# A decoder layer on one core: output projection of two blocks per weight group, residual in DRAM by pair, FFN operands and S5's second half at other planned times

## The chip, the cores and the metric

The kernel runs on one core of a Trainium2 chip. Five engines work side by side, each through its own instructions in a fixed order: TensorE (PE, with its weight loads PEld), VectorE (DVE), ScalarE (ACT), GpSimd (POOL) and SyncE (SP), which here issues nearly all DMA transfers. They meet through semaphores. The metric is the device time of one execution in microseconds.

## The reference

One layer over 2048 positions with 1024 channels. The input is normalised and projected. 512 columns go through S5 (32 groups, each a complex diagonal state, then GELU and a sigmoid GLU), the rest through an RG-LRU with a gate. Both outputs are normalised and projected together, the residual is added, and a SwiGLU FFN follows. The part that the change touches, shortened:

```python
z = jax.nn.gelu(y)                                  # y: S5's output
z = z * jax.nn.sigmoid(z @ w_glu + b_glu)           # the GLU
...
mix = jnp.concatenate([rms_norm(s5_out, s5_out_g), rms_norm(lru_out, lru_out_g)], axis=-1)
x = x + mix @ w_out
h2 = rms_norm(x, norm2_g)
x = x + (jax.nn.silu(h2 @ w_gate) * (h2 @ w_up)) @ w_down
return rms_norm(x, final_g)
```

All is in fp32. A product of fp32 operands is made of three matmuls: each operand is split in a high part and a remainder, and high by high, high by remainder and remainder by high are summed in PSUM.

## The kernel before, in words

**Tiling and stages.** Channels lie on the partitions. Positions go in four blocks of 512 (b = 0 to 3). For each block `in_tb` makes the input projection, the RG-LRU and S5's input. S5 runs twice, g = 0 for blocks 0 and 1, g = 1 for blocks 2 and 3, eight steps each: `s5_in`, `s5_scan`, `s5_out`; `s5_u` loads its input, `s5_z` stores its output to the DRAM tensor `zb`. Then `glu_tb(b)` makes the GLU of a block and its normalised mix, and `out_tb(b)` the output projection. The FFN works on pairs of blocks with a Winograd form of seven products (j = 1 to 7) on sums and differences of operand quarters.

**What sets the order.** Python code writes events with planned times (`at(t, fn)`) in units in which a product of three matmuls is PT = 0.65. The events are sorted by this time; a scheduler in the building layer then places each engine's instructions by its own model of when they are ready. So a planned time is a wish, and the order that comes out is fixed before the program runs.

**Around the change.** `Unit` (L152 to L205) loads a weight tile in parts of four chunks (`wraw`), splits each part on ACT (`whi`, L188) and on DVE or POOL (`wlo`, L189). `out_tb(b, t0)` makes eight units for the eight output chunks m, with 24 matmuls each (L214), out of the operands that `pair(b)` names: `areaH`/`areaL` (tiles `aH`, `aL`, in pool Q) for even blocks, `actH`/`actL` (pool A) for odd ones. Each product ends in one of two PSUM banks `acc`. L968 adds the residual `xc`, `SumSq` squares and sums it, and the result goes to the DRAM tensor `x1d`; at the end the row scale goes to `r2d`. The blocks follow one another: GLU 0 and 1, projection 0 and 1, GLU 2 and 3, projection 2 and 3. In `glu_tb`, `zsplit` splits GELU's output into `pair(b)`, and `mix(k)` writes the normalised operand k (0 to 3 from S5, 4 to 7 from the RG-LRU) to the same tiles: a DVE instruction (`nf`, L299), an ACT cast (L300) and a subtraction on DVE or POOL (L301).

The FFN's first operands come from `x_first(0, t)`: for k = 0 to 3, `combos` loads two chunks of `x1d` for both blocks of the pair and the row scales (three tiles `hx`, L1053 and L1055), normalises them (L1059), builds the Winograd sums `ht`, and `split_x2` splits them into `xh`, `xl`. `x_ahead(1)` does the same for the second pair later and stores the results to `xcd`. All these tiles belong to pool D1, which `open_d1` opens after it has closed pools L, Q and S; D1 takes over their space, and each tile waits until what lay there has been read.

Of the kernel before, what the change touches and what calls it, by code (L numbers as in the profile page):

```python
# [79 lines left out]
def build(tc, nc, I, O, ctx):  # L80
# [44 lines left out]
    x1d = dram("x1d", (DM, SEQ))  # L125
    r2d = dram("r2d", (SEQ,))
# [111 lines left out]
    class SumSq:  # L238
# [24 lines left out]
        @staticmethod  # L263
        def spread(y, dst=None):
            ps = aux("nm")
            if dst is not None:
# [4 lines left out]
                return
            for i in range(4):
                PE.matmul(ps[:, 128 * i:128 * i + 128], lhsT=y[:, i:i + 1].to_broadcast([128, 128]), rhs=eye,
                          start=True, stop=True)
# [593 lines left out]
    for g, (ts, dt) in enumerate(((ts0, 10), (tP1 - 10.0, 7))):  # L868
# [18 lines left out]
    def glu_tb(b, t0):  # L887
# [52 lines left out]
        t = t0 + 16 * PT  # L940

# [4 lines left out]
        for i, k in enumerate((4, 5, 6, 7)):  # L946
            at(max(t0 + 6.0, t2s) + 0.5 * i, lambda k=k: mix(k))
        at(t + 6.0, lambda: cur.__setitem__("rs", cur["ss"].finish()))
        for k in range(4):
            at(t + 7.0 + 0.5 * k, lambda k=k: mix(k))  # L950

    def out_tb(b, t0):
        cur = C[b]
        ss = SumSq(8, dv=b == NB - 1)
        for m in range(8):
            t = t0 + m * 8 * PT
            u = Unit(t, I["w_out"][m], 8, GP if m % 3 == 1 else DV)

            def prod(m=m, u=u):
                cur["o", m] = acc()  # L960
                mm3(cur["o", m], u, [(k, k) for k in range(8)], *pair(b), True, True)

            at(t - 5, lambda m=m: cur.__setitem__(("x", m), load_chunk(xT, b, m)))
            at(t, prod)

            def post(m=m):
                xc = cur.pop(("x", m))
                DV.tensor_tensor(out=xc, in0=cur.pop(("o", m)), in1=xc, op=ALU.add)  # L968
                ss.add(xc)
                SP.dma_start(x1d[128 * m:128 * m + 128, b * TB:(b + 1) * TB], xc)  # L970
# [10 lines left out]
    for kind, b in (("g", 1), ("o", 0), ("o", 1), ("g", 2), ("g", 3), ("o", 2), ("o", 3)):  # L981
        if kind == "g":
            glu_tb(b, T)
            T += 16 * PT
        else:
            out_tb(b, T)
            T += 64 * PT
# [57 lines left out]
    def combos(p, k, t):  # L1045

        o = 2 * TB * p
        cur = {}

        def load():  # L1050
            for i in range(2):
                cur[i] = d1("hx", 3, w=2 * TB)
                SP.dma_start(cur[i], x1d[128 * (k + 4 * i):128 * (k + 4 * i) + 128, o:o + 2 * TB])  # L1053
            rs = cur["rs"] = d1("hx", 3, w=2 * TB)
            SP.dma_start(rs, r2d[o:o + 2 * TB].unsqueeze(0).to_broadcast([128, 2 * TB]))  # L1055
# [184 lines left out]
    def down(t0):  # L1240
# [287 lines left out]
```

## Time and profile before

| | |
|---|---|
| median of 3 runs | 2169.43 us (2167.53 to 2169.79) |
| the profiled execution | 2175.18 us, span 2173.4 us |
| mean granted TensorE clock in it | 0.955 |
| input projections, RG-LRU, S5's first half and the start of its second | to about 440 us |
| S5's second half, GLU 1, first products of the projection | 440 to 600 |
| projection 0 and 1, GLU 2 and 3, projection 2 and 3 | 500 to 778 |
| FFN, gate and up, then down | from 778 |

The profile gives busy time per engine in a stretch, the granted TensorE clock (1.00 is full speed), and for each instruction the idle time before it and what ended it, in brackets. A wait on an engine other than TensorE matters only where TensorE runs out of work because of it.

### The profile page before, as it was taken

Reading aid. Unit: us, or ns where it says so; the run is one execution under the profiler, and the core shown is the slowest. Engines: PE = TensorE matmul, PEld = TensorE weight load, DVE = VectorE, ACT = ScalarE, POOL = GpSimd, SP = SyncE. Lnnn points to the kernel's source line nnn. Section 1 sums busy time; section 2 is a strip of 40 time slices with the busy share of each in tenths; the row PEclk is TensorE's granted clock in tenths of the full one; section 3 lists DMA queues with packets and bytes.
Section 4 is the critical chain, followed back from the end, with each engine's and each line's share of the span. In section 5 each row is a group of like instructions: output and inputs, shape, how many; then the busy total and the mean of one; then the engine's idle time right before and its main releaser. Section 6 shows DMA issues by size and latency. Waiting matters only on the chain.

```text
span 2173.4 us, 26158 instructions
## 1 busy us (share of the span) xinstructions
PE 1956.8 (90%) x8600; PEld 1564.3 (72%) x8600; DVE 1244.8 (57%) x1920; ACT 815.4 (38%) x1340; POOL 1042.6 (48%) x855
## 2 busy tenths in 40 slices
PE   6758989877898968899999989999999999999996
PEld 4536767666776756677777777777777788888785
DVE  5997658488856586444444464444444536554644
ACT  4534653563354342232332342232332344333331
POOL 1576236468834468545545552312313336544442
PEclk8968999988998989999999999999999999999998
DMA  7746998874772888644444574444443569854633
GB/s 293 218 153 190 297 248 273 226 179 142 226 209 94 257 264 279 200 146 146 160 146 143 172 235 134 149 131 136 145 131 126 189 224 317 279 184 135 232 102 102
DMA packets 264423, 413.61 MB, mean 190 GB/s; under 512 B 60736, under 2 KB 82528, under 8 KB 264288
## 3 DMA queue, kind: packets, MB, share of 16 engines
q1 hardware_dynamic: 264288, 411.95, 59.7%
q8 instruction: 67, 1.10, 0.2%
q14 instruction: 68, 0.56, 0.1%
HBM read 288.89 MB, written 122.96 MB: 189 GB/s over the span
## 4 chain that ended last, share of the span: by engine, by line
PE 55%; DVE 4%; DMA 4%; POOL 3%; issue 2%; ACT 1%; SPq 0%; POOLq 0%; DVEq 0%; ACTq 0%
PE gt L1184 9%; PE acc L1184 9%; PE y L1184 9%; PE v L1184 5%; PE nm L1184 5%; PE y L1324 4%; PE acc L1324 4%; PE gt L1324 4%; PE v L1324 2%; PE nm L1324 2%; PE acc L214 2%; DVE wlo L1024 1%; DMA ht<-xcd 1%; DVE hx L1059 1%; DMA wraw<-w_down 1%
## 5 line engine op out<-in xcount | busy, mean ns | idle before, releaser
L1197 POOL TENSOR_TENSOR t<-t 128x512 f32<-128x512 f32 x66 | 100.8, 1527 | 348.9 <-DVE t L1223 219.4
L214 PE MATMUL acc<-actH,whi 128*128 128x512 f32 x528 | 220.0, 418 | 43.5 <-DVE gy L710 12.1
L1023 ACT CAST whi<-ws 128x512 fp32r<-128x512 f32 x176 | 109.2, 621 | 346.9 <-PE y L1184 90.4
L214 PE MATMUL acc<-actL,whi 128*128 128x512 f32 x528 | 217.5, 413 | 18.8 <-DVE actL L294 17.8
L214 PE MATMUL acc<-actH,wlo 128*128 128x512 f32 x528 | 216.9, 412 | 6.9 <-DMA wlo<-wlc 6.9
L1024 DVE TENSOR_TENSOR wlo<-ht,whi 128x512 fp32r<-128x512 f32 x112 | 107.1, 957 | 126.3 <-ACT whi L1023 122.1
L214 PEld LDWEIGHTS acc<-actH,whi 128*128 128x128 f32 x528 | 105.9, 201 | 73.8 <-issue 24.8
L1023 ACT CAST whi<-ht 128x512 fp32r<-128x512 f32 x154 | 95.1, 619 | 169.9 <-PE nm L1324 69.5
L1024 DVE TENSOR_TENSOR wlo<-ws,whi 128x512 fp32r<-128x512 f32 x176 | 134.1, 762 | 33.7 <-ACT whi L1023 33.6
L1024 DVE TENSOR_TENSOR wlo<-wraw,whi 128x512 fp32r<-128x512 f32 x88 | 72.0, 818 | 142.2 <-ACT whi L1023 142.2
L1184 PE MATMUL y<-xh,whi 128*128 128x512 f32 x308 | 124.7, 405 | 16.2 <-ACT t L1216 12.0
L214 PEld LDWEIGHTS acc<-actL,whi 128*128 128x128 f32 x528 | 105.1, 199 | 46.7 <-DVE actL L294 24.7
L1024 POOL TENSOR_TENSOR wlo<-ht,whi 128x512 fp32r<-128x512 f32 x42 | 57.9, 1379 | 158.9 <-ACT whi L1023 158.9
L1184 PE MATMUL acc<-xh,wlo 128*128 128x512 f32 x308 | 122.3, 397 | 9.6 <-DVE wlo L1024 9.6
L214 PEld LDWEIGHTS acc<-actH,wlo 128*128 128x128 f32 x528 | 105.2, 199 | 30.6 <-DMA wlo<-wlc 7.4
L1184 PE MATMUL acc<-xh,whi 128*128 128x512 f32 x308 | 122.4, 397 | 4.6 <-ACT xh L1023 3.3
L1184 PE MATMUL y<-xl,whi 128*128 128x512 f32 x308 | 123.3, 400 | 3.5 <-DVE xl L1024 3.5
L1184 PE MATMUL y<-xh,wlo 128*128 128x512 f32 x308 | 123.3, 400 | 2.9 <-DVE wlo L1024 2.9
L1184 PE MATMUL acc<-xl,whi 128*128 128x512 f32 x308 | 122.2, 397 | 1.7 <-DVE xl L1024 1.7
L1184 PE MATMUL gt<-xh,whi 128*128 128x512 f32 x308 | 121.4, 394 | 0.0
L1184 PE MATMUL gt<-xh,wlo 128*128 128x512 f32 x308 | 121.3, 394 | 0.0
L1184 PE MATMUL gt<-xl,whi 128*128 128x512 f32 x308 | 121.2, 394 | 0.0
(416 smaller groups left out, 5308.0 us busy)
## 6 DMA issues: line engine op xcount, KB each, us to landing
td<-t SPq DMA_DIRECT2D x154, 256.0 KB, 2.2
ht<-td SPq DMA_DIRECT2D x154, 256.0 KB, 3.0
wraw<-w_down SPq DMA_DIRECT2D x99, 256.0 KB, 4.5
wraw<-w_in SPq DMA_DIRECT2D x96, 256.0 KB, 5.2
scd<-ws SPq DMA_DIRECT2D x88, 256.0 KB, 2.1
ws<-scd SPq DMA_DIRECT2D x88, 256.0 KB, 2.6
wlo<-wlc SPq DMA_DIRECT2D x72, 256.0 KB, 4.4
wraw<-w_out SPq DMA_DIRECT2D x64, 256.0 KB, 4.5
```

What stands on the lines that cost most here:

```text
L214: PE.matmul(ps, lhsT=part[w][:, kw % 4, :], rhs=r_(x(kx)), start=first and i == 0 and j == 0, stop=last and i == n - 1 and j == 2)
L1023: AC.copy(hi, raw)
L1024: eng.tensor_tensor(out=lo, in0=raw, in1=hi.bitcast(F32), op=ALU.subtract)
L1059: DV.scalar_tensor_tensor(out=cur[i], in0=cur[i], scalar=pc("g2", k + 4 * i), in1=cur["rs"], op0=ALU.mult, op1=ALU.mult)
L1184: PE.matmul(ps, lhsT=a[:, k, :], rhs=x, start=j in FIRST and k == 0 and i == 0, stop=k == 3 and i == 2, skip_group_check=True)
L1197: (DV if q == 0 else GP).tensor_tensor(out=g, in0=c, in1=g, op=ALU.mult)
L1324: PE.matmul(BK[p][i], lhsT=a[:, i, :], rhs=x, start=j in FIRST and s == 0 and v == 0, stop=s == NSL - 1 and v == 2, skip_group_check=True)
```

## The change

`out_tb` becomes `out_pair(b0, t0)`. It makes the eight units of `w_out` once for two blocks. For blocks 0 and 1 the products go: chunks 0 and 1 of block 0, chunks 0 and 1 of block 1, then chunks 2 to 5 with the blocks alternating; after a planned gap of 32 PT, in which `glu_tb(2)` and `glu_tb(3)` stand, chunks 6 and 7 of block 0, then of block 1. For blocks 2 and 3 chunks 0 and 1 go the same way and chunks 2 to 7 alternate. Products end in four banks, two `acc` and two `gt`, in pairs. Each block has its own sum tile (`sum`, `sumh`); `rs` has two buffers instead of three.

`x1d` and `r2d` become two DRAM tensors each, one for a pair. GLU 2 and 3 split GELU's output into a tile `zhl` of its own (tag `u8`, one buffer, S5's input tile before), since `pair(b)` is still being read; their mix has a planned time `tm` after products 6 and 7. The RG-LRU operands of odd blocks take the tags `T` and `ig`. S5's second half is planned 16 later (tP1 + 6 instead of tP1 - 10), `open_d1` and `x_first(0)` 128 PT ahead of the FFN instead of 64.

```diff
-    for g, (ts, dt) in enumerate(((ts0, 10), (tP1 - 10.0, 7))):
+    for g, (ts, dt) in enumerate(((ts0, 10), (tP1 + 6.0, 7))):
...
+        def zpair():
+            if b < 2:
+                return pair(b)
+            if "zhl" not in cur:
+                zz = bt("u8", (128, 2, 4, TB))
+                cur["zhl"] = tuple((lambda k, i=i: zz[:, i, k, :]) for i in range(2))
+            return cur["zhl"]
...
-            at(max(t0 + 6.0, t2s) + 0.5 * i, lambda k=k: mix(k))
+            at((max(t0 + 6.0, t2s) if b < 2 else tm - 2.0) + 0.5 * i, lambda k=k: mix(k))
...
+    def out_bank():
+        n = last["bank"] = last.get("bank", -1) + 1
+        return acc() if n % 4 < 2 else aux("gt", 2)
+
+    def out_pair(b0, t0):
+        sums = {b: SumSq(8, ("sum", "sumh")[b % 2], dv=b >= NB - 2) for b in (b0, b0 + 1)}
+        blocks = (b0, b0 + 1)
+        order = [(m, b) for b in blocks for m in (0, 1)]
+        order += [(m, b) for m in range(2, 6 if b0 == 0 else 8) for b in blocks]
+        if b0 == 0:
+            order += [(m, b) for b in blocks for m in (6, 7)]
+        units = {}
+        for n, (m, b) in enumerate(order):
+            cur = C[b]
+            t = t0 + n * 8 * PT + (32 * PT if b0 == 0 and n >= 12 else 0)
+            if m not in units:
+                units[m] = Unit(t, I["w_out"][m], 8, GP if m % 3 == 1 else DV)
...
+    glu_tb(1, T)
+    T += 16 * PT
+    out_pair(0, T)
+    tg = T + 96 * PT
+    glu_tb(2, tg, T + (128 + 16 + 1) * PT)
+    glu_tb(3, tg + 16 * PT, T + (128 + 32 + 1) * PT)
+    T += 128 * PT + 32 * PT
+    out_pair(2, T)
+    T += 128 * PT
...
-    at(tC - 64 * PT + 4.0, open_d1)
+    at(tC - 128 * PT + 4.0, open_d1)
     at(tC + 1.0, open_d2)
-    x_first(0, tC - 64 * PT + 12.0)
+    x_first(0, tC - 128 * PT + 12.0)
```

Three places in the order that comes out. First TensorE where the first two products end, before (`acc_4508` is chunk 1 of block 0, `acc_4634` its chunk 2; `y` and `v` are steps of S5):

```order
L863 MATMUL y_4389<-u8_3797,mo_4196 128x128
L259 MATMUL nm_4541<-ones_62,sumg_4335 128x1 x4
L214 MATMUL acc_4400<-aL3_4104,whi_4355 128x512
L214 MATMUL acc_4400<-aH3_4102,wlo_4356 128x512
L214 MATMUL acc_4508<-aL3_4104,whi_4475 128x512
L214 MATMUL acc_4508<-aH3_4102,wlo_4476 128x512
L801 MATMUL v_4485<-u8_3797,mi_4479 64x128 x8
L214 MATMUL acc_4634<-aH0_3624,whi_4504 128x512
L214 MATMUL acc_4634<-aL0_3626,whi_4504 128x512
```

and now, where `gt_4480` and `gt_4553` are chunks 0 and 1 of block 1:

```order
L863 MATMUL y_4542<-u8_3983,mo_4346 128x128
L801 MATMUL v_4628<-u8_3983,mi_4624 64x128 x8
L214 MATMUL gt_4480<-actH_70,whi_4126 128x512
L214 MATMUL gt_4553<-actH_70,whi_4239 128x512
L214 MATMUL gt_4480<-actL_71,whi_4126 128x512
L214 MATMUL gt_4480<-actH_70,wlo_4127 128x512
```

The third product was block 0's and is now block 1's, in other banks, and its first matmuls alternate with the fourth's. Second DVE, before, at block 3's first product (`xc_6116` takes it out of its bank, `xc_6160` is the second's; `hx`, `xl10`, `ht` belong to `x_first`, k = 0):

```order
L968 TENSOR_TENSOR xc_6116<-acc_6135,xc_6116 128x512
L189 TENSOR_TENSOR wlo_6242<-wraw_6118,whi_6241 128x512
L1059 SCALAR_TENSOR_TENSOR hx_6245<-hx_6245,par_61,hx_6249 128x1024
L1059 SCALAR_TENSOR_TENSOR hx_6247<-hx_6247,par_61,hx_6249 128x1024
L226 TENSOR_SCALAR nv_6180<-nm_6175 128x4
L1024 TENSOR_TENSOR xl10_6314<-hx_6245,xh10_6313 128x512
L1068 TENSOR_TENSOR ht_6298<-hx_6247,hx_6245 128x512
L228 TENSOR_SCALAR nv_6180<-nv_6180 128x4
L189 TENSOR_TENSOR wlo_6254<-wraw_6129,whi_6253 128x512
L1069 TENSOR_TENSOR ht_6299<-ht_6298,hx_6245 128x512
L229 TENSOR_SCALAR nv_6180<-nv_6180 128x4
L1024 TENSOR_TENSOR xl70_6326<-ht_6298,xh70_6325 128x512
```

and now, where `acc_6332` is chunk 6 of block 3, `gt_6374` and `gt_6416` are chunk 7 of blocks 2 and 3, the last product:

```order
L990 TENSOR_TENSOR xc_6319<-acc_6332,xc_6319 128x512
L253 TENSOR_TENSOR sumh_5875<-sumh_5875,sq_6402 128x512
L990 TENSOR_TENSOR xc_6359<-gt_6374,xc_6359 128x512
L253 TENSOR_TENSOR sum_5760<-sum_5760,sq_6442 128x512
L990 TENSOR_TENSOR xc_6399<-gt_6416,xc_6399 128x512
L1082 SCALAR_TENSOR_TENSOR hx_5763<-hx_5763,par_61,hx_5767 128x1024
L1082 SCALAR_TENSOR_TENSOR hx_5765<-hx_5765,par_61,hx_5767 128x1024
L226 TENSOR_SCALAR nv_6458<-nm_6453 128x4
L253 TENSOR_TENSOR sumh_5875<-sumh_5875,sq_6494 128x512
L1048 TENSOR_TENSOR xl10_5820<-hx_5763,xh10_5819 128x512
```

`x_first` stood between block 3's products and now stands behind all of them. Third SP at the same place, before:

```order
L182 DMA wraw_6173<-w_out 128x512
L1053 DMA hx_6245<-x1d_84 128x1024
L1053 DMA hx_6247<-x1d_84 128x1024
L970 DMA x1d_84<-xc_6072 128x512
L1055 DMA hx_6249<-r2d_85 128x1024
L182 DMA wraw_6235<-w_out 128x512
```

and now:

```order
L992 DMA x1d1_85<-xc_6319 128x512
L1076 DMA hx_5763<-x1d0_84 128x1024
L1076 DMA hx_5765<-x1d0_84 128x1024
L1078 DMA hx_5767<-r2d0_86 128x1024
L1155 DMA rd_6361<-w_gate 128x512
L992 DMA x1d1_85<-xc_6359 128x512
```

`xc_6072` is block 2's eighth product, `xc_6319` block 3's seventh: the loads stood ahead of the store of block 2's last product, with block 3's eight still to come, and now stand behind the store of the third product from the end.

More of the change, by code (lines that the diff above doesn't have):

```diff
@@ L124, in build @@
     lrud = dram("lrud", (512, SEQ))
-    x1d = dram("x1d", (DM, SEQ))
-    r2d = dram("r2d", (SEQ,))
+    x1d = [dram(f"x1d{i}", (DM, 2 * TB)) for i in range(2)]
+    r2d = [dram(f"r2d{i}", (2 * TB,)) for i in range(2)]
     xcd = dram("xcd", (2, 4, 128, 7, TB))
@@ L926, in prod @@
                     mm3(cur["ps", 2 * uu + i], u, [(4 * i + k, k) for k in range(4)],
-                        *pair(b), True, True)
+                        *zpair(), True, True)
             at(t, prod)
@@ L940, in glu_tb @@
         t = t0 + 16 * PT
+        tm = t + 7.0 if tm is None else tm
         def mix(k):
@@ L946, in glu_tb @@
         for i, k in enumerate((4, 5, 6, 7)):
-            at(max(t0 + 6.0, t2s) + 0.5 * i, lambda k=k: mix(k))
+            at((max(t0 + 6.0, t2s) if b < 2 else tm - 2.0) + 0.5 * i, lambda k=k: mix(k))
         at(t + 6.0, lambda: cur.__setitem__("rs", cur["ss"].finish()))
         for k in range(4):
[L950 to L960, printed above, removed]
+            at(tm + 0.5 * k, lambda k=k: mix(k))
@@ L961, in prod, with post @@
                 mm3(cur["o", m], u, [(k, k) for k in range(8)], *pair(b), True, True)
[L963 to L966 removed]
+            def post(m=m, b=b, cur=cur):
                 xc = cur.pop(("x", m))
                 DV.tensor_tensor(out=xc, in0=cur.pop(("o", m)), in1=xc, op=ALU.add)
[L969 to L970 removed]
+                sums[b].add(xc)
+                SP.dma_start(x1d[b // 2][128 * m:128 * m + 128, TB * (b % 2):TB * (b % 2) + TB], xc)
@@ L972, in out_tb @@
+            at(t - 5, lambda m=m, b=b, cur=cur: cur.__setitem__(("x", m), load_chunk(xT, b, m)))
+            at(t, prod)
             at(t + 8 * PT + 0.5, post)
-        def fin():
-            ss.finish(r2d[b * TB:(b + 1) * TB])
-        at(t0 + 64 * PT + 4.0, fin)
+            if m == 7:
+                at(t + 8 * PT + 4.0, lambda b=b: sums[b].finish(r2d[b // 2][TB * (b % 2):TB * (b % 2) + TB]))
     glu_tb(0, tin[3] + 64 * PT + 5.3)
     T = tP1 + 16 * PT
[L981 to L987, printed above, removed]
+    glu_tb(1, T)
@@ L1052, in load @@
                 cur[i] = d1("hx", 3, w=2 * TB)
-                SP.dma_start(cur[i], x1d[128 * (k + 4 * i):128 * (k + 4 * i) + 128, o:o + 2 * TB])
+                SP.dma_start(cur[i], x1d[p][128 * (k + 4 * i):128 * (k + 4 * i) + 128])
             rs = cur["rs"] = d1("hx", 3, w=2 * TB)
-            SP.dma_start(rs, r2d[o:o + 2 * TB].unsqueeze(0).to_broadcast([128, 2 * TB]))
+            SP.dma_start(rs, r2d[p].unsqueeze(0).to_broadcast([128, 2 * TB]))
         def norm():
@@ L1329, in load_row @@
             x = tmp()
-            m, o = i + 4 * (q // 2), TB * (2 * p + q % 2)
-            SP.dma_start(x, x1d[128 * m:128 * m + 128, o:o + TB])
+            m, o = i + 4 * (q // 2), TB * (q % 2)
+            SP.dma_start(x, x1d[p][128 * m:128 * m + 128, o:o + TB])
             return x
```

13 lines of the change are left out of this document (7 added, 6 removed).

## The prediction

> **What bounds the kernel now.** I read the page's first part, then the windows view of the stretch that the change touches, then single waits there.
>
> ```profile
> PE 1956.8 (90%) x8600; PEld 1564.3 (72%) x8600; DVE 1244.8 (57%) x1920; ACT 815.4 (38%) x1340; POOL 1042.6 (48%) x855
> ...
> 440.00:500.00 60.00, 49.79 (x264) 39.67 (x263) 55.19 (x83) 34.08 (x51) 45.51 (x53) 0.89 0.63 170
> 500.00:550.00 50.00, 39.37 (x190) 29.94 (x189) 43.26 (x76) 16.60 (x32) 43.50 (x52) 0.90 0.54 168
> 560.00:620.00 60.00, 52.29 (x252) 42.97 (x251) 36.30 (x61) 19.52 (x34) 38.89 (x44) 0.94 0.71 204
> 640.00:705.00 65.00, 55.59 (x236) 43.59 (x235) 43.44 (x75) 29.72 (x51) 30.44 (x22) 0.89 0.35 111
> 705.00:740.00 35.00, 35.00 (x157) 28.45 (x157) 11.29 (x17) 11.19 (x19) 12.76 (x10) 1.00 0.75 236
> 740.00:777.00 37.00, 33.22 (x139) 26.57 (x138) 35.33 (x42) 15.47 (x28) 25.82 (x16) 0.95 0.88 288
> 777.00:801.00 24.00, 11.10 (x37) 6.71 (x35) 21.66 (x29) 6.21 (x12) 16.79 (x10) 0.74 0.69 223
> 801.00:880.00 79.00, 57.62 (x215) 43.75 (x216) 50.42 (x49) 23.55 (x40) 58.47 (x38) 0.87 0.83 275
> ...
> 889.80 2.80 PE acc L1184 x12
> ```
>
> The columns after the stretch and its width are the busy time of PE, PEld, DVE, ACT and POOL, then the granted clock. TensorE is the bound wherever it is fed: 12 matmuls take 2.80 us, a product of 24 takes 5.6. The change keeps every matmul, so time can only come from what TensorE loses. I count that as width minus busy time times clock: 15.7, 14.6 and 10.8 in the first three rows, 15.5 in 640 to 705, 0 in 705 to 740, 5.4, 15.8 and 28.9 in the last three. The first three rows are S5's second half beside the projection's first products, 640 to 705 is GLU 2 and 3 ahead of their projection, 740 to 801 the FFN's first operands.
>
> Single waits say what ends the idle time:
>
> ```profile
> 535.55 0.62 PE L214 MATMUL acc<-aH,whi 128*128 128x512 f32 x1 [2.80 <-DVE xc L968]
> 583.90 0.77 PE L214 MATMUL acc<-actH,whi 128*128 128x512 f32 x1 [4.32 <-DVE xc L968]
> 674.03 1.22 PE L214 MATMUL acc<-aH,whi 128*128 128x512 f32 x2 [4.38 <-ACT aH L300]
> ```
>
> Two are a product that waits for one of two PSUM banks, the third is a mix operand of block 2 that comes late.
>
> **The FFN's first operands: the term that decides.** The edit asks for them 128 PT ahead instead of 64. What lets them start is memory:
>
> ```profile
> 727.00 0.39 PE L214 MATMUL acc<-aH,wlo 128*128 128x512 f32 x1
> 727.23 0.39 PE L214 MATMUL acc<-actH,whi 128*128 128x512 f32 x1
> ...
> 727.69 0.90 SPq L1053 DMA_DIRECT2D hx<-x1d  x2
> ...
> 729.25 0.79 SPq L1055 DMA_DIRECT2D hx<-r2d  x1
> ...
> 737.33 2.48 DVE L1059 SCALAR_TENSOR_TENSOR hx<-hx,par 128x1024 f32<-128x1024 f32 x2 [3.15 <-DMA hx<-r2d]
> 755.20 2.48 DVE L1059 SCALAR_TENSOR_TENSOR hx<-hx,par 128x1024 f32<-128x1024 f32 x2
> 774.08 4.57 DVE L1059 SCALAR_TENSOR_TENSOR hx<-hx,par 128x1024 f32<-128x1024 f32 x2
> 795.43 2.48 DVE L1059 SCALAR_TENSOR_TENSOR hx<-hx,par 128x1024 f32<-128x1024 f32 x2
> ...
> 799.63 0.80 PE L1184 MATMUL y<-xl,whi 128*128 128x512 f32 x1 [1.42 <-DVE xl L1024]
> ```
>
> `hx` lies in the pool D1, which takes over the space of pool Q, where `aH` and `aL` of block 2 live. The first load issues 0.5 us after the last matmul on `aH`. Block 3's 64 PT of products, out of `actH`, then cover what follows: the last `acc<-actH` matmul ends near 778, 51 us after the release. In the changed kernel blocks 2 and 3 alternate, so `aH` is read until the last product but one. The order shows the consequence: on SP the first `hx` load stands behind the store of the third product from the end, and on DVE the first `hx` instruction stands behind the evacuation of the very last one. The cover shrinks from 51 us to about 7.
>
> Call E the end of the last product. `hx` becomes free in pieces during the last product but one, from E-10 to E-7. What follows is four rounds, one for each k, that cannot overlap: three `hx` buffers serve a round that needs three. Its prices:
>
> ```profile
> hx<-x1d SPq DMA_DIRECT2D x16, 512.0 KB, 5.1
> hx<-r2d SPq DMA_DIRECT2D x8, 512.0 KB, 5.7
> xcd<-hx SPq DMA_DIRECT2D x16, 256.0 KB, 3.5
> ht<-td SPq DMA_DIRECT2D x154, 256.0 KB, 3.0
> ...
> 744.48 0.68 DVE L1024 TENSOR_TENSOR xl<-ht,xh 128x512 fp32r<-128x512 f32 x1
> 802.55 1.76 DVE L1024 TENSOR_TENSOR wlo<-ws,whi 128x512 fp32r<-128x512 f32 x1
> ...
> L301 POOL TENSOR_TENSOR aL<-nf,aH 128x512 fp32r<-128x512 f32 x6 | 8.6, 1441 | 0.2
> ```
>
> Round 1: the r2d load goes out near E-6.5 and took 8.1 us before (729.25 to 737.33), so its normalisation starts at E+1. Until the next r2d load can go, POOL runs seven instructions of 1.4 us behind the first half of the normalisation (five are weight sums and splits that the order puts between), 1.2 + 9.8 = 11 us; 5.7 more for the load: round 2 starts 17 us later, at E+18. Before it took 17.9. Rounds 2 and 3 have little between: normalisation 2.5, three DVE instructions of 0.68 and a POOL one of 1.4, some 6.5 with the handovers, and 5.7 for the load: 12 us each, where 18.9 and 21.3 were seen with the projection's evacuations and weight splits on the same DVE. Round 4 starts at E+42, its first operands are split 3 us later, E+45. Until then TensorE has 18 matmuls of the rounds before, 4 us. It loses 41, and about 2 more since it restarts on a low clock (0.74 in 777 to 801, and 0.80 us for a matmul that takes 0.39 at speed). Before, the same step cost 15.8. So the term is **+27**. Bounds: loads at the 3.0 us of a quiet queue and a first round of 13 us give E+33, a loss of 31 and +15; rounds as long as before, 17.9, 18.9 and 21.3, give E+62, a loss of 60 and +44. I take 27, since rounds 2 and 3 plainly lose their company and loads of 512 KB have never been seen near 3.0.
>
> The Trainium skill, "TensorE: Matmul & The Clock Gate", Part 1, says that the clock is halved after an idle window of about 3.4 us and returns after as much steady work, so one long idle stretch pays it about once or twice; the 0.74 agrees, and by the page alone the surcharge would be some 2 us for each long wait.
>
> What comes after, 801 to 880, loses 28.9: `x_ahead(1)`, the weight sums and the first stores to `td` queue up on POOL and SP. Their order is the same in both kernels, so 0, between -10 (weights of two groups are made while TensorE idles) and +5.
>
> **S5 and the first products.** S5's rows stand on PE at nearly the same places as before; 16 us of planned delay moved them little, and the glu and mix steps past them. What changes is that the third and fourth product are now block 1's, and so need block 1's mix. DVE is what those wait for:
>
> ```profile
> L299 DVE SCALAR_TENSOR_TENSOR nf<-r,par,xq 128x512 f32<-128x512 f32 x14 | 13.7, 987 | 5.8 <-POOL aL L301 3.7 <-DMA xq<-rld 2.1
> L840 DVE TENSOR_TENSOR_SCAN s_ta<-lamb,s_k,s_wr 128x128 f32<-128x128 f32 x16 | 13.4, 873 | 1.3 <-POOL s_wr L810 1.3
> L189 DVE TENSOR_TENSOR wlo<-wraw,whi 128x512 fp32r<-128x512 f32 x15 | 15.7, 1045 | 1.2 <-ACT whi L188 1.2
> ...
> 526.24 0.63 PE L862 MATMUL y<-s_s,mo 128*128 128x128 f32 x2
> ...
> 549.75 0.39 PE L862 MATMUL y<-s_s,mo 128*128 128x128 f32 x2
> ...
> 487.37 2.05 PE L273 MATMUL nm<-eye,nv 128*128 128x128 f32 x8 [5.11 <-DVE nv L234]
> ```
>
> From 500 to 550 DVE does 76 instructions in 50 us, 0.66 us each. From block 0's row scale (487.4) to the first evacuations the order has 69 of them before, 45 us, and the trace says 48 (535.55). Now there are 52 to the first two evacuations and 51 more to the next two: 68 us, 555. Four more products at 5.6 bring the eighth to 578; before, the eighth was done at 583.9 - 4.3 = 579.6. So nothing is won or lost up to there. Half of the weight splits are gone (of the 16 parts of eight products 8 remain), which is in the counts.
>
> Behind it, four PSUM banks instead of two end the wait of 4.32 us and its slow matmuls, some 8 of the 10.8 us lost from 560 to 620. But GLU 2 now comes right behind S5:
>
> ```profile
> 599.28 0.63 PE L863 MATMUL y<-u,mo 128*128 128x128 f32 x2
> ...
> 617.01 1.28 ACT L150 ACT_TABLE_LOAD   x1 [4.77 <-DMA zA<-zb]
> 618.31 1.92 ACT L150 ACTIVATE zA<-zA 128x2048 f32<-128x2048 f32 x1
> ...
> 620.64 2.17 ACT L911 CAST aH<-zA 128x512 fp32r<-128x512 f32 x4
> ```
>
> From S5's last output (599.9) over the stores to `zb`, the loads, the Gelu and the first split is 21 us. Before, 50 us of other matmuls lay between. Now 72 matmuls do, 16.8 us: 4.5 of waiting and some 1.5 on a low clock. Sum of the stretch: -8 + 6 = **-2**, between -11 (all that 560 to 620 lost) and +10 (S5 half a step later; the two outputs at 526 and 550 are a step of 23 us apart).
>
> **GLU 2 and 3.** Their statistics and mix (15.5 lost) now have products 6 and 7 of blocks 0 and 1 beside them. Block 2's mix may begin when block 0's last product has read `aH`; 34 matmuls, 8 us, cover its 7 us to the first operand, and eight steps of 0.99 plus half as many splits fill 11 us against 11.2 of products. Block 3's follows the same way and comes some 5 late; `zhl` has one buffer, so GLU 3's split waits for GLU 2's matmuls, 2 us; 2 for the clock. Loss 9: **-6**, between -15.5 and 0.
>
> **The second pair's products** are dense with four banks: the 5.4 of 740 to 777 go, **-5** (0 to -5.4). 32 weight loads, 32 ACT casts, 20 DVE and 12 POOL splits that fall away lie beside TensorE and count only through these terms.
>
> **Sum**: +27 + 0 - 2 - 6 - 5 = +14. The profiled execution took 2175.2 us (span 2173.4), the median of the runs is 2169.4, 5.8 less; I put the sum on the median: **2183 us**.
>
> **The rivals.** *A short prologue and a good projection (faster).* If a round costs 9.5 (loads at 3.0) instead of 12 and 17, E+33, the prologue is +15, and if the projection's three gains come near their ends (-11, -12, -5) the sum is -13: 2156. It turns where the fourth round's operands are ready by E+31 with the gains as forecast, by E+46 with all of them. For it: SP and the 16 DMA engines are emptier there than in the trace of before. Against: 5.7 for r2d is the median, not the worst. [...]
>
> *S5 late, GLU 2 held (slower still).* One S5 step more, or zb's stores behind waiting entries on SP, makes the 4.5 us into 20: 2199. For it: POOL is 87% busy in 500 to 550. Against: S5's rows end at the same place on PE.
>
> *The operands really are made beside the projection.* Then 15.8 goes as well: 2169 - 16 - 13 = 2140. Against it stands the order of DVE; 4%.
>
> **Chances.** The forecast, +5 to +35: 0.57. Slower still: 0.07. Between -4 and +4, the two groups cancelling: 0.13. Faster by the short prologue 0.19, by the last rival 0.04. A measurement of this kernel tells about 0.2%, 4.3 us, from no change. Slower 0.64, same 0.13, faster 0.23. Range 2158 to 2203: the prologue at its lower bound, +15, with 26 of the 28 that can be gained, up to the prologue at its upper bound, +44, with 10 gained.
>
> **What would show it.** In the changed profile: a stretch of over 35 us behind the last projection product with few matmuls and `hx<-r2d` as releaser, `hx` normalisations about 17, 12 and 12 apart; a dense projection ahead of it, without waits for `xc`; one wait of some 5 us at GLU 2's first matmul, released over `zA`. Wrong if the `hx` loads issue before the last product but one, if the rounds are under 10 us, or if 480 to 620 grows by more than 10.

## The result, and the profile after

The changed kernel takes 2198.9 us (median of 4 runs, 2196.5 to 2202.8) against 2169.6 us of the kernel before in the same comparison: a ratio of 1.0137, 95% interval 1.0117 to 1.0157. It is slower by 29.3 us. The direction was forecast, and the time lies inside the range; the size, +14, was less than half of it.

The first line of the changed kernel's page has less work on ACT, DVE and POOL than before and the same on TensorE (instructions 1340, 1920 and 855 before; the 32 splits that fall away are 13 on DVE and 19 on POOL, where the prediction had 20 and 12):

```profile
PE 1961.2 (89%) x8600; PEld 1560.2 (71%) x8600; DVE 1231.4 (56%) x1907; ACT 800.1 (36%) x1308; POOL 1011.1 (46%) x836
```

The windows view of the changed kernel, columns as in the prediction (stretch, width, PE, PEld, DVE, ACT, POOL busy, granted clock, DMA share, GB/s). Its last projection product ends at 766:

```profile
440.00:500.00 60.00, 51.39 (x250) 40.93 (x247) 56.01 (x74) 34.30 (x52) 47.74 (x47) 0.89 0.60 171
500.00:550.00 50.00, 32.32 (x186) 24.26 (x186) 42.10 (x86) 12.59 (x26) 41.65 (x59) 0.86 0.61 172
560.00:620.00 60.00, 56.83 (x290) 45.81 (x289) 25.46 (x44) 23.79 (x36) 28.98 (x36) 1.00 0.64 179
620.00:700.00 80.00, 71.99 (x307) 54.60 (x306) 53.77 (x93) 32.76 (x56) 32.85 (x24) 0.96 0.29 89
700.00:766.00 66.00, 66.00 (x288) 53.23 (x286) 20.70 (x34) 13.44 (x22) 5.41 (x5) 1.00 0.48 155
766.00:835.00 69.00, 25.51 (x64) 13.76 (x62) 52.13 (x61) 19.16 (x34) 40.91 (x25) 0.55 0.60 200
835.00:900.00 65.00, 47.32 (x187) 36.63 (x187) 39.70 (x39) 17.39 (x29) 50.03 (x33) 0.91 0.81 277
900.00:940.00 40.00, 38.73 (x156) 30.98 (x157) 17.96 (x25) 10.70 (x18) 23.10 (x17) 0.93 0.56 191
```

Two stretches of the kernel before that the prediction does not show are needed to compare the whole:

```profile
620.00:640.00 20.00, 18.32 (x81) 14.88 (x80) 13.75 (x17) 14.58 (x26) 9.97 (x8) 1.00 0.72 202
...
880.00:920.00 40.00, 38.99 (x168) 31.22 (x167) 17.71 (x24) 11.89 (x20) 22.69 (x17) 0.99 0.58 196
```

Counted as in the prediction (width minus busy time times clock), TensorE loses:

| stretch | before | after | difference | forecast |
|---|---|---|---|---|
| S5 and the first products, to 620 | 15.7 + 14.6 + 10.8 = 41.1 | 14.3 + 22.2 + 3.2 = 39.7 | -1.4 | -2 |
| GLU 2 and 3, 620 to 705 (after: 700) | 1.7 + 15.5 = 17.2 | 10.9 | -6.3 | -6 |
| second pair's products | 5.4 | 0 | -5.4 | -5 |
| FFN's first operands (before 777 to 801, after 766 to 835) | 15.8 | 55.0 | +39.2 | +27 |
| what comes behind (before to 920, after to 940) | 28.9 + 1.4 = 30.3 | 21.9 + 4.0 = 25.9 | -4.4 | 0 |
| sum | | | +21.7 | +14 |

From 550 to 560 neither loses anything.

Of the waits that the prediction named, the one for `xc` is not found any more from 500 to 766, and GLU 2's first matmul waits 0.95 us where some 5 were forecast. New is a wait of 8.67 us for block 1's row scale, with which its mix begins:

```profile
533.27 2.04 PE L273 MATMUL nm<-eye,nv 128*128 128x128 f32 x8 [8.67 <-DVE nv L234]
...
608.73 0.73 PE L214 MATMUL acc<-u,whi 128*128 128x512 f32 x2 [0.95 <-ACT u L920]
```

The two profiled executions differ by 2196.96 - 2175.18 = 21.8 us, about the table's sum. The agreement is better than the count: the clock has two digits, and the same count gives some 2 us less lost ahead of 440 and some 3 less behind the table. The medians differ by 7.5 us more: the profiled execution before was 5.6 us slower than its median, the one after 2.0 faster. Where those 7.5 us lie no trace shows. They are within the spread of single executions: those of the kernel before run from 2164.4 to 2176.8 in the comparisons below.

**Inside the prologue.** The DVE rows of the changed kernel (start, duration, engine, line, tile, idle time before and its releaser):

```profile
766.80 2.52 DVE L1082 SCALAR_TENSOR_TENSOR hx<-hx,par 128x1024 f32<-128x1024 f32 x2
...
774.30 1.23 DVE L228 TENSOR_SCALAR nv<-nv 128x4 int32<-128x4 int32 x1
...
789.97 0.16 DVE L226 TENSOR_SCALAR nv<-nm 128x4 f32<-128x4 f32 x1 [2.98 <-PE nm L259]
...
792.15 0.16 DVE L234 SCALAR_TENSOR_TENSOR nv<-nv 128x4 f32<-128x4 f32 x1
792.24 2.48 DVE L1082 SCALAR_TENSOR_TENSOR hx<-hx,par 128x1024 f32<-128x1024 f32 x2
794.64 1.76 DVE L1048 TENSOR_TENSOR xl<-hx,xh 128x512 fp32r<-128x512 f32 x1
...
805.45 2.48 DVE L1082 SCALAR_TENSOR_TENSOR hx<-hx,par 128x1024 f32<-128x1024 f32 x2 [4.30 <-DMA hx<-r2d]
...
818.85 2.48 DVE L1082 SCALAR_TENSOR_TENSOR hx<-hx,par 128x1024 f32<-128x1024 f32 x2 [4.49 <-DMA hx<-r2d]
```

and the SP queue's issues of the row loads of rounds 2 to 4:

```profile
780.76 0.33 SPq L1078 DMA_DIRECT2D hx<-r2d  x1
...
800.63 0.32 SPq L1078 DMA_DIRECT2D hx<-r2d  x1
...
813.84 0.32 SPq L1078 DMA_DIRECT2D hx<-r2d  x1
```

The rounds start 25.4, 13.2 and 13.4 us apart, where 17, 12 and 12 were forecast. Rounds 3 and 4 are the forecast chain with other parts: 8.4 us from a normalisation to the next row load (6.5 forecast) and 4.8 and 5.0 to its landing (5.7 forecast). The 8.4 are long because two of the three DVE instructions between take 1.76 us (the row at 794.64 is one) where 0.68 was taken. Round 2 is another case. Its normalisation has no wait of its own: it stands on DVE behind the row scales of blocks 2 and 3 (`nv`), and block 3's waits 2.98 us for TensorE's sum, which stands behind block 2's on TensorE.

On TensorE dense products begin later than round 4's first operand is split (823.0):

```profile
826.39 0.80 PE L1207 MATMUL y<-xh,whi 128*128 128x512 f32 x1 [2.11 <-ACT t L1239]
```

The bank `y` had to be emptied by ACT first. Dense products begin at 826.4, 60 us behind the last projection product; the forecast had 45.

**Behind the prologue.** The waits of TensorE from 855 to 905 (total, times, longest), and two DVE rows there:

```profile
PE acc L1207 <- DVE wlo L1048: 8.7, 1, 8.7
PE nm L1207 <- DVE wlo L1048: 3.7, 1, 3.7
PE y L1207 <- DVE wlo L1048: 2.9, 1, 2.9
```

```profile
896.05 2.48 DVE L1082 SCALAR_TENSOR_TENSOR hx<-hx,par 128x1024 f32<-128x1024 f32 x2 [9.10 <-DMA hx<-r2d]
898.45 1.75 DVE L1048 TENSOR_TENSOR wlo<-wraw,whi 128x512 fp32r<-128x512 f32 x1
```

A weight remainder that TensorE needs is ready to be made, but stands behind a normalisation of `x_ahead(1)` that waits 9.1 us for its row load. The change did not bring these waits: in the kernel before TensorE has the same three from 801 to 880, of 9.6, 3.4 and 2.2 us.

### The profile page after: what moved, and what is told of

Same layout as the page of the kernel before. It is cut to its first block, busy times and chain, and to the rows that moved or that the text cites. A ratio compares the mean times of both kernels' runs of the same rounds, so it can differ in the third digit from the quotient of the medians.

```text
span 2195.2 us, 25944 instructions
## 1 busy us (share of the span) xinstructions
PE 1961.2 (89%) x8600; PEld 1560.2 (71%) x8600; DVE 1231.4 (56%) x1907; ACT 800.1 (36%) x1308; POOL 1011.1 (46%) x836
## 4 chain that ended last, share of the span: by engine, by line
PE 63%; DVE 15%; DMA 8%; POOL 4%; ACT 4%; issue 4%; SPq 1%; POOLq 0%; DVEq 0%; ACTq 0%
PE acc L1207 9%; PE gt L1207 9%; PE y L1207 9%; PE acc L214 7%; PE v L1207 5%; PE nm L1207 5%; PE y L1347 4%; PE acc L1347 4%; PE gt L1347 3%; PE gt L214 3%; PE nm L1347 2%; PE v L1347 2%; DVE xh L661 1%; DMA wraw<-w_in 1%; DVE nf L299 1%
## 5 line engine op out<-in xcount | busy, mean ns | idle before, releaser
L214 PE MATMUL acc<-actH,whi 128*128 128x512 f32 x424 | 177.3, 420 | 34.5 <-DVE gy L710 10.5
L214 PE MATMUL acc<-actL,whi 128*128 128x512 f32 x424 | 176.7, 418 | 21.3 <-DVE actL L294 19.9
L214 PE MATMUL acc<-actH,wlo 128*128 128x512 f32 x424 | 175.2, 415 | 4.2 <-DMA wlo<-wlc 3.9
L1207 PE MATMUL y<-xh,whi 128*128 128x512 f32 x308 | 126.5, 411 | 27.9 <-ACT xh L1047 13.3
L214 PEld LDWEIGHTS acc<-actH,whi 128*128 128x128 f32 x424 | 85.6, 202 | 58.1 <-issue 17.4
L214 PEld LDWEIGHTS acc<-actL,whi 128*128 128x128 f32 x424 | 84.9, 200 | 46.2 <-DVE actL L294 26.3
L1047 ACT CAST whi<-wraw 128x512 fp32r<-128x512 f32 x88 | 54.6, 621 | 156.3 <-PE y L1207 53.0
```

Source lines behind the costliest of these rows:

```text
L214: PE.matmul(ps, lhsT=part[w][:, kw % 4, :], rhs=r_(x(kx)), start=first and i == 0 and j == 0, stop=last and i == n - 1 and j == 2)
L1047: AC.copy(hi, raw)
L1207: PE.matmul(ps, lhsT=a[:, k, :], rhs=x, start=j in FIRST and k == 0 and i == 0, stop=k == 3 and i == 2, skip_group_check=True)
```

## The experiments

Times are medians; each ratio is to the kernel before, run beside it. "After" is the changed kernel. A difference to it is one between two comparisons, and by their intervals good to some 5 us. Where an expectation puts the prologue's loss at 61 us, the table's count, 766 to 835, gives 55.0.

**The lost cover: the address or the order.** In the first, `open_d1` requests D1's tiles once in another sequence, so that each gets another address:

```diff
         D["1"] = sD1.enter_context(tc.tile_pool(name="D1", bufs=1, reuse_waits="tile"))
+        def xt(k):
+            for j in (1, 6, 2, 7, 4):
+                for c in "hl":
+                    xtile(c, j, k)
+        for k in (3,):
+            xt(k)
+        for _ in range(5):
+            D["1"].tile([128, 4, 128], F32, tag="ws", name="ws", bufs=5)
+        for k in (2, 1, 0):
+            xt(k)
```

> The changed kernel, with pool D1's tiles laid out in another order: `hx` now lies over S5's matrices and the end of GLU 3's split, which have been read by about 690 us; the tiles over `aH` and `aL` are operands of the fourth and third round and the weight sums. The order on every engine stays the same: the `hx` loads stand on SP behind the store of the third product from the end. Theory of the address (the prediction's: `hx` waits while the program runs, until `aH` under it has been read): the second chunk and the row load no longer wait 2.9 us; the prologue of 61 us lost begins up to 3 us earlier, 2194. Theory of the order (the space of a closed pool is given out only when all of it is free, so the order fixed beforehand puts `x_first` behind the projection, and the address is not what ends the wait): 2197, no change, as DVE's first normalisation stands behind the last evacuation anyway. A fall of more than 10 us speaks against both.

2200.2 us, ratio 1.0141 (1.0124 to 1.0158). Its first row load on SP and its second normalisation on DVE:

```profile
756.83 0.43 SPq L1088 DMA_DIRECT2D hx<-r2d  x1
```

```profile
791.87 2.48 DVE L1092 SCALAR_TENSOR_TENSOR hx<-hx,par 128x1024 f32<-128x1024 f32 x2
```

The load goes 2.6 us earlier (759.47 in the changed kernel), round 2 starts 0.4 earlier. So the address held the loads back by 2.6 us, which gains nothing; it is not what puts the rounds behind the projection. The second experiment leaves pool Q open:

```diff
     def open_d1():
         sL.close()
-        sQ.close()
         sS.close()
...
+        if (j, k) in HOLD:
+            if c == "h":
+                n = HOLD.index((j, k))
+                held[j, k] = Q.tile([128, 2, TB], dt, tag=f"pc{n % 2}{n // 2}", name=name or tag)
+            return held[j, k][:, "hl".index(c), :]
...
+    HOLD = ((1, 3), (6, 3), (2, 3), (7, 3), (4, 3), (2, 2), (7, 2), (4, 2))
```

> The changed kernel, but pool Q, which holds `aH` and `aL`, stays open: D1 lies beside it, over pools L and S, which are free when block 3's mix is done (about 705 us), and eight pairs of FFN operands (all of the fourth round, three of the third) take Q's tiles one by one. The order now puts the four rounds between the second pair's products, and the same instructions are run. Theory (the 61 us lost in the prologue come from the lost cover alone): the prologue loses 5 to 15 instead of 61, and the projection beside it loses up to 5: 2145, 2138 to 2158, faster than the kernel before the change (2169). Rival (the rounds take DVE, ACT, POOL and DMA time from the dense projection, 705 to 766, or the FFN's start waits for its weight sums in any case): 2165 to 2185.

2149.3 us, ratio 0.9904 (0.9888 to 0.9919): 50 us less than the changed kernel, and faster than the kernel before. Three of its four normalisations now stand between the products, and its last product ends at 768.8 (first and fourth):

```profile
715.28 2.48 DVE L1088 SCALAR_TENSOR_TENSOR hx<-hx,par 128x1024 f32<-128x1024 f32 x2 [1.81 <-DMA hx<-r2d]
...
772.89 2.48 DVE L1088 SCALAR_TENSOR_TENSOR hx<-hx,par 128x1024 f32<-128x1024 f32 x2 [1.78 <-DMA hx<-r2d]
```

```profile
700.00:768.00 68.00, 67.49 (x293) 54.11 (x293) 52.30 (x60) 22.58 (x40) 34.12 (x21) 1.00 0.77 253
768.00:835.00 67.00, 52.82 (x201) 39.44 (x200) 47.34 (x69) 22.75 (x40) 37.83 (x25) 0.82 0.65 221
835.00:900.00 65.00, 57.74 (x236) 45.14 (x235) 37.34 (x39) 17.16 (x30) 54.25 (x36) 0.95 0.78 275
```

The prologue loses 67 - 52.82 x 0.82 = 23.7 instead of 55.0, more than the 5 to 15 expected, since round 4 comes too late; the stretch behind loses 10.1 instead of 21.9, with waits on `wlo` of 1.0 us instead of 15.3. So the time fell in the expected range partly by a gain that the theory did not have. Beside the rounds the projection stays dense (0.5 lost), so the rival of contention falls.

**Only blocks 2 and 3 apart.**

```diff
             order += [(m, b) for b in blocks for m in (6, 7)]
+        else:
+            order = [(m, b) for b in blocks for m in range(8)]
...
-            if m not in units:
+            if m not in units or b0 and b == b0 + 1:
```

> The changed kernel, but blocks 2 and 3 are projected one after the other, each with its own eight weight units, as before the change; everything else is as changed, with the planned time of `x_first` too. Theory: `aH` and `aL` are free after block 2's last product, block 3's eight products cover three of the four rounds again, and the prologue loses about 16 as before the change: 61 - 16 = 45 less, 16 more weight loads beside it for 0 to 5: 2154, 2147 to 2162. Rival (the long prologue comes from the planned time or the delayed S5, not from the alternation of blocks 2 and 3): 2190 or more.

2150.0 us, ratio 0.9908 (0.9891 to 0.9925), the theory's time, but made up otherwise:

```profile
766.00:777.00 11.00, 6.96 (x24) 4.75 (x22) 11.00 (x8) 3.51 (x6) 10.27 (x6) 0.85 0.71 246
777.00:835.00 58.00, 41.37 (x149) 30.24 (x150) 46.84 (x55) 21.09 (x36) 38.93 (x24) 0.82 0.75 251
835.00:900.00 65.00, 60.20 (x256) 47.42 (x256) 39.85 (x41) 17.71 (x31) 56.91 (x37) 1.00 0.81 285
```

From 766 to 835 it loses 5.1 + 24.1 = 29.2 instead of 55.0, where the theory had 16; behind that it loses 4.8 instead of 21.9, where the theory had no gain. The alternation of blocks 2 and 3 alone makes the change slow, through the cover and through the order behind it. The planned time of `x_first` has no part in it: with 64 PT in place of 128 the order on every engine comes out the same, so that was not run.

**The cover by one product.**

```diff
+        else:
+            order = order[:-4] + [(m, b) for b in blocks for m in (6, 7)]
```

> The changed kernel with the last four products of blocks 2 and 3 in the order that blocks 0 and 1 have: chunks 6 and 7 of block 2, then 6 and 7 of block 3. `aH` and `aL` are free one product (5.6 us) earlier, and the `hx` loads and the first normalisation stand one product earlier in the order. Theory (each us of cover takes one us from the prologue): 5.6 less, 2192, 2189 to 2195. Rival (the row scales and loads between set the length, the cover does not): 2196 to 2200.

2178.3 us, ratio 1.0048 (1.0029 to 1.0067): 21 us less, where 5.6 were expected. First and last normalisation of the four rounds, and the windows:

```profile
760.90 2.48 DVE L1084 SCALAR_TENSOR_TENSOR hx<-hx,par 128x1024 f32<-128x1024 f32 x2
...
813.15 2.48 DVE L1084 SCALAR_TENSOR_TENSOR hx<-hx,par 128x1024 f32<-128x1024 f32 x2 [4.11 <-DMA hx<-r2d]
```

```profile
766.00:835.00 69.00, 30.06 (x81) 17.57 (x80) 53.59 (x65) 22.49 (x38) 41.21 (x26) 0.60 0.60 207
835.00:900.00 65.00, 56.77 (x236) 44.64 (x235) 45.17 (x44) 18.07 (x32) 54.32 (x34) 0.97 0.82 280
```

The rounds are 5.9 and 5.7 us earlier, one to one; the prologue's window loses 51.0 instead of 55.0. The larger part, 9.9 instead of 21.9, comes from behind it, where the order of weights and `x_ahead(1)` came out otherwise: the waits on `wlo` there are 0.9 us instead of 15.3.

**The row scale ahead of round 2.** `rsqrt` gets an argument `skip`, true for the row scales of blocks 2 and 3:

```diff
+        if skip:
+            v = P.tile([128, 3, w_], F32, tag=f"nv{w_}", name="nv", bufs=2)
+            AC.copy(v[:, 0, :], ss)
+            return v[:, 0, :]
```

> The changed kernel without the Newton steps of the row scales of blocks 2 and 3: ScalarE copies the sums instead, so the second pair's scale is not computed. On DVE 24 instructions of 0.15 to 1.25 us, which stand between the first and the second round's normalisations, fall away, and with them the wait for TensorE's second sum. Theory (the second round, at E+26 where E+18 was forecast, is late by that row scale, since its row load lands near E+21): 5 to 7 us less, 2191. Rival (the loads set the round): 2196 to 2198.

2192.4 us, ratio 1.0102 (1.0084 to 1.0120), 6.5 less. Round 2:

```profile
785.87 2.48 DVE L1086 SCALAR_TENSOR_TENSOR hx<-hx,par 128x1024 f32<-128x1024 f32 x2 [2.57 <-DMA hx<-r2d]
```

Round 2 starts 6.4 us earlier, and now its row load is what it waits for. The time alone would not show it, since the intervals of the two ratios touch; the trace does.

**DVE behind the prologue.**

```diff
-            for i in range(2):
+            for i in range(2 if p == 0 else 0):
                 DV.scalar_tensor_tensor(out=cur[i], in0=cur[i], scalar=pc("g2", k + 4 * i), in1=cur["rs"],
```

> The changed kernel without the normalisations of `x_ahead(1)`, eight DVE instructions of 1.3 us (the second pair's FFN input is left unnormalised); its loads, sums and stores stay. Theory (behind the prologue, 860 to 900, TensorE waits three times, 15.3 us in all, for weight remainders that stand on DVE behind such a normalisation, and that one waits up to 9 us for its row load): 12 to 15 less, 2184, 2181 to 2188. Rival (the weight sums come late from POOL in any case): 2193 to 2199.

2176.3 us, ratio 1.0024 (1.0008 to 1.0040): 23 less by the medians, more than expected. The profiled execution, the slowest of its 11 at 2182.85, is 14.1 less than the changed kernel's, as expected. In its window behind the prologue TensorE loses 1.6:

```profile
840.00:900.00 60.00, 58.45 (x249) 46.07 (x248) 37.91 (x42) 22.67 (x39) 56.60 (x38) 1.00 0.94 347
```

The three waits on `wlo` are gone, though POOL is busier than in the changed kernel (56.6 of 60 against 50.0 of 65). The normalisations that stand on DVE waiting for a load cost 14 to 23 us there; the edit takes away their own 10 us of DVE time too, and does not tell the two apart.

**The other parts of the change.** S5's time back:

```diff
-    for g, (ts, dt) in enumerate(((ts0, 10), (tP1 + 6.0, 7))):
+    for g, (ts, dt) in enumerate(((ts0, 10), (tP1 - 10.0, 7))):
```

> The changed kernel with S5's second half planned at tP1 - 10 again, as before the change. Theory (the prediction's: 16 us of planned delay hardly move S5's rows and are worth nothing): 2197, 2193 to 2201. Rival (the delay is what lets the first products run without waits, 7 us less lost at 600 than before the change): 2202 to 2208.

2199.9 us, ratio 1.0139 (1.0123 to 1.0155): the delay is worth nothing. Two banks:

```diff
-        return acc() if n % 4 < 2 else aux("gt", 2)
+        return acc()
```

> The changed kernel with two PSUM banks for the projection's products instead of four. Theory (the prediction's: four banks end the waits for evacuations, and the measured gains, 7 us up to 600 and 6 from 740 on, come from them): 10 to 13 us more, 2209, 2204 to 2213. Rival (the pairs of products in a new order end the waits, the banks do nothing): 2197, 2194 to 2200.

2200.5 us, ratio 1.0148 (1.0128 to 1.0168), between the two, nearer the rival's number; its interval includes the changed kernel's. The prediction let the banks carry -8 and -5, but with two of them the stretch of that wait loses 3.9, and before the change it lost 10.8; the second pair's products, 700 to 766, lose nothing with two banks either:

```profile
560.00:620.00 60.00, 56.12 (x277) 44.94 (x275) 23.12 (x41) 20.73 (x31) 30.84 (x37) 1.00 0.60 176
```

No gap (the mix of blocks 2 and 3 goes back behind their statistics, `open_d1` is planned 5 later and `x_first` 3):

```diff
-            t = t0 + n * 8 * PT + (32 * PT if b0 == 0 and n >= 12 else 0)
+            t = t0 + n * 8 * PT
...
-    tg = T + 96 * PT
-    glu_tb(2, tg, T + (128 + 16 + 1) * PT)
-    glu_tb(3, tg + 16 * PT, T + (128 + 32 + 1) * PT)
+    tg = T + 128 * PT
+    glu_tb(2, tg)
+    glu_tb(3, tg + 16 * PT)
```

> The changed kernel without the gap: chunks 6 and 7 of blocks 0 and 1 come right behind the others, and GLU 2 and 3 with their mix stand behind them alone, as before the change (`open_d1` is planned 5 later for it). Theory (products 6 and 7 cover the mix of blocks 2 and 3; the windows show only 2 us less lost from 620 to 700 than before the change, where 6 were forecast): 2 to 6 us more, 2201. Rival (the cover brings nothing, since these products wait for the same weights and DVE): 2195 to 2198.

2183.8 us, ratio 1.0061 (1.0044 to 1.0078), 15 less: neither theory. Its windows:

```profile
620.00:705.00 85.00, 73.86 (x310) 58.11 (x309) 61.06 (x100) 37.37 (x64) 32.29 (x24) 0.88 0.28 90
...
771.00:840.00 69.00, 25.68 (x62) 13.88 (x62) 53.01 (x63) 20.99 (x36) 40.16 (x25) 0.55 0.60 198
840.00:900.00 60.00, 52.99 (x213) 41.69 (x212) 43.46 (x41) 18.19 (x31) 50.39 (x32) 0.94 0.81 281
```

GLU 2 and 3 lose 20.0 instead of 10.9, so the gap does what was forecast of it. The prologue is the same, 54.9. Behind it 10.2 are lost instead of 21.9: again the order there, without a wait on `wlo`. The rest of the 15 us was not placed.

**What the change is worth when the prologue is covered.** First the kernel before with the edit of e2_area_kept, and nothing else:

> The kernel before the change, with pool Q kept open as in e2_area_kept and nothing else: the order now lets the four rounds begin when pools L and S are free (about 705) instead of when block 2 is projected (727). Theory (the prologue is set by when the space is free, here too): its loss of 15.8 falls to about 3, and `x_ahead` behind it starts earlier for another 5: 2150, 2143 to 2160, so as fast as e2_area_kept; the pairing itself is then worth little. Rival (before the change the rounds are set by their own work beside the projection, 18 to 21 us each, not by the release): 2163 to 2169.

2145.3 us, ratio 0.9886 (0.9870 to 0.9902). Its rounds begin at 708 and the fourth at 760, 25 us ahead of the end of its last product, 784.5, and nearly all of the prologue is gone (5.1 lost):

```profile
785.00:835.00 50.00, 44.91 (x196) 35.42 (x195) 39.95 (x50) 19.75 (x34) 33.29 (x22) 1.00 0.74 253
```

The change with the edits of e2_area_kept and e10_no_gap:

> e2_area_kept without the gap (as e10_no_gap): block 1's row scale is ready before GLU 2, so the first three rounds can begin some 10 us earlier than in e2_area_kept. Theory (what is left of e2_area_kept's prologue, some 25 us lost, is its fourth round, whose operands lie in Q's tiles and wait for `aH` and `aL` to be read): the projection loses 4 more, the prologue the same, 2150, 2145 to 2156. Rival (the rounds' late begin behind block 1's row scale is what is left): 2135 to 2143.

2145.2 us, ratio 0.9894 (0.9875 to 0.9913): at the edge of the theory, and apart from neither it nor the rival by its interval. The trace speaks for the theory: round 4's normalisation is at 771.95 again, behind the last product, though the first three rounds begin earlier. The same with the edit of e3_blocks_apart too:

> Pool Q kept open, no gap, and blocks 2 and 3 projected apart: of the change only the pairing of blocks 0 and 1 and the four banks are left. All four rounds now stand beside the projection, as in e5_before_kept, and the fourth is not held by Q's tiles. Theory (the pairing saves the projection some 10 us, 208 to 212 lost at its end against 222 before the change, and that stays when the prologue is short): e5_before_kept, 2145, less 10: 2136, 2131 to 2140. Rival (with the prologue short, the saved weight work is hidden anyway): 2143 to 2148.

2139.9 us, ratio 0.9867 (0.9845 to 0.9889), at the upper edge of the theory, with an interval that reaches into the rival's range. Round 4 now begins at 750.76. So the pairing was taken out as well, on one chip beside a second run of the same kernel:

```diff
-        order = [(m, b) for b in blocks for m in (0, 1)]
-        order += [(m, b) for m in range(2, 6 if b0 == 0 else 8) for b in blocks]
...
+        order = [(m, b) for b in blocks for m in range(8)]
```

> e16_apart_kept with blocks 0 and 1 projected apart too, each with its own eight weight units: no pairing anywhere, but four banks, the delayed S5 and the open pool Q. Theory (pairing blocks 0 and 1 saves the projection 8 to 10 us that nothing hides): 8 to 10 us more than e18_apart_kept_again, 2148. Rival (with the prologue short the halved weight work is hidden beside TensorE): within 3 us of it, 2141.

> The same kernel as e16_apart_kept, beside e17_all_apart_kept on the same chip, for the comparison of the two: 2140, 2136 to 2144, as it was there; both theories expect that.

2142.6 us, ratio 0.9867 (0.9845 to 0.9889), without any pairing; 2142.3 us, ratio 0.9866 (0.9844 to 0.9888), with blocks 0 and 1 paired. There is no difference. Why, the windows of e17 (first) and e18 show:

```profile
500.00:550.00 50.00, 41.66 (x228) 31.66 (x229) 46.83 (x88) 17.92 (x36) 43.72 (x57) 0.97 0.61 193
560.00:620.00 60.00, 52.00 (x259) 42.01 (x258) 35.49 (x66) 16.38 (x34) 39.22 (x51) 0.94 0.66 194
```

```profile
500.00:550.00 50.00, 33.59 (x181) 26.25 (x180) 40.41 (x86) 12.36 (x26) 41.00 (x59) 0.83 0.58 174
560.00:620.00 60.00, 60.00 (x307) 49.26 (x306) 25.53 (x44) 20.79 (x32) 30.66 (x37) 1.00 0.62 179
```

The pairing takes away the 11.1 us that are lost from 560 to 620, and loses 22.1 instead of 9.6 from 500 to 550, where the third product needs block 1's mix and TensorE stands at its row scale (the row at 533.27 of the changed kernel). These two, e5, e11 and e16 are within their intervals of each other; they are the fastest versions, 1.1 to 1.3% under the kernel before.

## Why the prediction had the direction right and the size wrong

**Where the size went.** The medians moved by 29.3 us where +14 was forecast. Of the 15 us between, the FFN's first operands are 12; the stretch behind them gave 4 back, the other terms fit within 1, and 7.5 lie between the profiled executions and the medians.

**Right: what decides, and the projection.** The FFN's first operands lost their cover: the `hx` loads and the first normalisation stand where the prediction put them, the stretch of over 35 us is there, and its loss outweighs the rest. The three terms of the projection, -2, -6 and -5, measured -1.4, -6.3 and -5.4. The first was right in sum with a wrong reason: the gain from 560 to 620 comes with the pairs of products (e17 loses it, e8 with two banks keeps most of it), not with four banks, and the price from 500 to 550 is the wait at the head of block 1's mix, which the prediction named and priced at nothing up to the eighth product. The third has the same flaw: 700 to 766 is dense with two banks too (e8), while four banks without any pairing (e17) lose 5.2 from 700 to 777. GLU 2 was covered better than forecast (0.95 us for 4.5).

**Failed: the term +27 of the FFN's first operands.** Four serial rounds of three `hx` buffers came as forecast, and rounds 3 and 4 were paced by the row load; the length of the rounds was mis-sized, and round 2 waited for something else. E+18 for round 2 became E+26: the prediction counted POOL's seven instructions and the load, and left out the row scales of blocks 2 and 3 on the same DVE, 24 instructions and a wait for TensorE. Their first row stands in the order that is shown with the change, right behind `hx_5765`, and e4 prices them at 6.4 in its trace. The rest is POOL, whose seven instructions took 12.5 us instead of 9.8. Rounds of 12 became 13.3, 2.6 us more, for the DVE instructions of 1.76 us. From round 4's normalisation to dense products it is 7.5 us (818.85 to 826.39) where 3 were taken, since the first products also wait for ACT to empty the bank `y`. Together 8 + 2.6 + 4.5 = 15 us later, of which the window shows 12 as loss, +39 instead of +27. The upper bound, +44, held. The lower bound has a slip in its sum: it leaves out the 3 us to the first split that the forecast and the upper bound count, and with them is E+36 and +18.

**Held, but no constant: what comes after, 0.** The argument was that its order is the same in both kernels. It measured -4.4 here, inside its bounds, and the same three waits on `wlo` stand in both. What the runs show beyond it is that the term moves easily: 1.6, 4.8, 9.9, 10.2 and 21.9 us are lost in that window with orders that differ by little (e12, e3, e13, e10, after). What decides is whether weight remainders stand on DVE behind a normalisation whose load has not landed.

**Right effect, wrong cause: "what lets them start is memory".** The prediction took the address: `hx` lies on `aH`. With `hx` elsewhere (e1) the order and the time stay; with the pool kept open (e2) the rounds move 46 to 63 us ahead. What holds the rounds back is the closing of the whole pool, in the order fixed before the program runs. How the building layer decides that was not looked at; that the planned time has no part in it is seen from the unchanged order at 64 PT.

**The median.** The sum was put on the median, with the profiled execution 5.8 us above it. Against the profiled execution the change is +21.8, against the medians +29.3. Nothing run here explains the 7.5 between them, beyond the spread of single executions. Had they not come, the size would have been short by 8 and not by 15.

**The rivals.** "A short prologue" needed operands at E+31; dense products began at E+60. "S5 late, GLU 2 held" did not occur: its time, 2199, was met for another reason. "The operands really are made beside the projection" did not come in this kernel, as the order of DVE had said, and is what e2, e5 and e16 then did: 2149 to 2140, near its 2140.

## What to carry to other kernels

Ask of each early start what gates it: the planned time, the data, the address, or the pool. Here a pool that closes late cost 39 us in one stretch, three times what the projection had gained, and leaving it open was worth 1.1% to the kernel that had not been changed at all. When a stretch loses its cover, count every instruction on each in-order engine between its steps, also those that belong to another chain (the row scales, 6.5 us); and do not put a load's consumer ahead of other work on an in-order engine (14 to 23 us behind the prologue, in a stretch where the kernel before had the same waits).

## What the runs showed of the hardware that was not expected

A small DVE instruction can wait for POOL's instruction to end. In the changed kernel's prologue the shift of line 228 on 128x4 numbers took 1.23 us at 774.30 and ended at 775.53; POOL was in a subtraction from 773.79 to 775.50. With POOL idle the same shift took 0.17 us, at 790.17. All six `nv` rows of over 1 us there end within 0.03 us of the end of one of POOL's rows, so the price is what POOL's instruction has left, and not a factor. The row of line 226, which reads PSUM, took 0.15 us at 769.25 inside one of POOL's rows:

```profile
769.25 0.15 DVE L226 TENSOR_SCALAR nv<-nm 128x4 f32<-128x4 f32 x1
...
790.17 0.17 DVE L228 TENSOR_SCALAR nv<-nv 128x4 int32<-128x4 int32 x1
```

```profile
768.28 2.18 POOL L1090 TENSOR_TENSOR ht<-hx 128x512 f32<-128x512 f32 x1 [1.23 <-DVE hx L1082]
...
773.79 1.71 POOL L1048 TENSOR_TENSOR xl<-hx,xh 128x512 fp32r<-128x512 f32 x1
...
793.61 2.25 POOL L1090 TENSOR_TENSOR ht<-hx 128x512 f32<-128x512 f32 x1 [7.41 <-DVE hx L1082]
```

The larger ones go the same way: the DVE row of 1.76 us at 794.64 ended 0.54 us after POOL's row at 793.61 (which ended at 795.86), and one of its size with POOL idle took 0.69 (798.19). That is what made rounds 3 and 4 longer than forecast.

The Trainium skill, "GPSIMD Engine Reference", section 8, says that the two engines share their SBUF interfaces and contend where a DVE instruction has two SBUF inputs or runs in a mode with two ports; that the row from PSUM goes free agrees with it. Whether the shift, with its one SBUF input, runs in such a mode no run shows. So the instructions of such a chain are priced by whether POOL works beside them: the 24 of the two row scales would take 4 us at 0.16 each, an estimate for an idle POOL.
